# Moving transfers of a two-layer decoder step to ScalarE's DMA queue, and two cache copies to the middle of the last stage

## The chip, the cores and the metric

The kernel runs on one core of a Trainium2 chip. Five engines work side by side, each through its own instructions in order: TensorE (PE, with PEld for its weight loads), VectorE (DVE), ScalarE (ACT), GpSimd (POOL) and SyncE (SP), which only issues DMAs here. A DMA is an instruction on the engine that issues it: if it must wait for a tile to be free or for data to be ready, whatever stands behind it on that engine waits too. "SPq" and "ACTq" in the profile are DMA issues by SP and ScalarE.

The metric is the device time of one execution in microseconds (us). A second figure, the span, is the part of one profiled execution between its first and last instruction.

## What is computed

The reference is one inference step of a two-layer decoder on a prompt of 2048 tokens and a sample group of 8 x 4 tokens, in f32. Cut to what matters:

```python
for layer in range(DEPTH):                       # DEPTH = 2
    if layer < N_A_LAYERS:                       # mixer A: gated linear attention
        dp, st_p = gla_mixer(hp, zero_state, *w)
        ds, st_s = gla_mixer(hs, state_gla[i], *w)
        hp, hs = hp + dp, hs + ds
        k_p, v_p = shared_kv(hp, kv_norm, w_k, w_v, k_norm, pos_p)
        k_new, v_new = shared_kv(hs, kv_norm, w_k, w_v, k_norm, pos_s)
        k_s = jnp.concatenate([cache_swa_k, k_new], axis=1)
        v_s = jnp.concatenate([cache_swa_v, v_new], axis=1)
    else:                                        # mixer B: sliding-window attention
        q_p, g_p = swa_query(hp, b_norm[j], b_w_in[j], b_q_norm[j], pos_p)
        hp = hp + swa_out(swa_banded(q_p, k_p, v_p, b_sinks[j]), g_p, b_w_out[j])
        q_s, g_s = swa_query(hs, b_norm[j], b_w_in[j], b_q_norm[j], pos_s)
        hs = hs + swa_out(attend(q_s, k_s, v_s, pos_s, kpos_s, b_sinks[j]), g_s, b_w_out[j])

def swa_out(o, gate, w_out):                     # the last stage: (2048 x 2048) @ (2048 x 1024)
    return (o.reshape(bsz, seq_len, BRANCH_WIDTH) * jax.nn.silu(gate)) @ w_out

# also returned, besides hp and hs: the states of mixer A, the last keys and values of the prompt, and
new_cache_swa_k_sample = k_s[:, seq_s:]          # the old cache without its first 4 rows, then 4 new rows
new_cache_swa_v_sample = v_s[:, seq_s:]
```

## The kernel before

All products run in pairs of f16 numbers (a high and a low part), three passes for one f32 product. Activations are held transposed, 128 tokens (a chunk) at a time; there are 16 chunks.

The stages follow one another in this order:

1. **Mixer A**, four heads of four blocks of 512 tokens. Its gated result goes out to DRAM as `ogd[c]`, one tensor for each chunk.
2. **Mixer A's output product** (`a_out`, L1052). For each chunk four transposed loads (L1059, `v` or `sg` <- `ogd`) bring the result back with the contracted dimension on the partitions; two products of 48 matmuls follow, into the banks `pj` and `o`; VectorE adds the residual (L1066), the sum `h` is stored as `hd[c]` (L1067), and `norm_T` (L298) squares, scales, splits and transposes it for mixer B into `uT`. Beside this run the steps of the list `prep`: they load the weights of mixer B, convert them to pairs and store them in DRAM. Last in that list is `form_steps` (L849): the output weights of mixer B are combined for a product in Strassen's manner, with seven products in place of eight. For each of eight block rows it loads four raw tiles (L857, into two tiles `wraw` and the tiles `qT` and `kT`), forms seven combinations on GpSimd (L864), splits each on ScalarE and VectorE (L197, L198) and stores it as `wfd[n]` by GpSimd's queue.
3. **Mixer B's attention**, four groups of 16 chunks, `ORDER` (L1522) interleaving the scores and values of one chunk with the projections of a later one. The probabilities are transposed by DMA through SP (L1285, `sth` and `pst` <- `v`). The result goes to DRAM as `ogd2[c]`. The attention of the samples lies between the groups.
4. **The passage to the last stage**, the last loop steps `n = TOT` to `TOT + 2` with `TOT` = 64: TensorE still works on the attention of the last chunks and fills in with the first products of the last stage. The lists `trickle` and `summing` hand out loads of factors and of blocks, and VectorE's sums, a step at a time.
5. **The last stage**, mixer B's output product, a `Pair` of two chunks at a time. For a pair, four blocks `x` = 0 to 3 are loaded transposed (L1569, `load` and `fetch`), VectorE and ScalarE build the operands of the seven products from them (`sums`), and TensorE runs seven products of 24 matmuls each (`PRODS`) with the factors `wf[0]` to `wf[6]`. Factors come by `wform_big` (L1533, a tile of the ring `uT`) or `wform` (L1538, four tiles of the ring `W`). `Pair.y` finishes one half chunk: it loads the residual (L1625), VectorE adds it (L1626) and the product (L1618), and the result is stored (L1627). `b_finish_s` (L1664 to L1670) does the same for the samples.

What sets the order: the program is written in the order above with priorities (`behind` lowers one), and a planner then arranges the instructions of each engine by its own estimate of their times. So an instruction may be issued far ahead of the place where it is written. TensorE's order alone is fixed to that of the program while `pin[0]` is set, from the start of mixer B to the end of the passage. `later` (L108) keeps a DMA in its place in program order. Tiles are rings of buffers: a tag with `bufs` = 2 gives the third user the first one's memory, and a write into it waits until the last reader is done.

Places that the change touches: the raw loads (L857); the residual and the results (L1625, L1627, L1667, L1670); the copies of the caches without their first rows (two DMAs from DRAM to DRAM by L108) and of the sixteen pieces with the new rows (L1748, from `kvS`), all written after the loop of the passage; the blocks 0 and 1 of pair 0, which are loaded at `TOT - 11` into a shared tile of the ring `uT` for the early products and once more by `pairs[0].load` for the sums; and the steps at which the factors 2 and 6 are loaded.

Of the kernel before, what the change touches and what calls it, by code (L numbers as in the profile page):

```python
# [19 lines left out]
P = 128  # L20
# [10 lines left out]
NS, TS = 8, 4  # L31
SMP = NS * TS
WIN = 128
# [41 lines left out]
def _body(tc, nc, cp, sb, ps, dr, i, o):  # L75
# [6 lines left out]
    def T(tag, shape, dt, bufs=None):  # L82
        return sb.tile(shape, dt, tag=tag, name=nm(tag), **({} if bufs is None else {"bufs": bufs}))
# [4 lines left out]
    def C(tag, shape, dt):  # L88
        return cp.tile(shape, dt, tag=tag, name=tag)
# [16 lines left out]
    def later(dst, src, q=nc.sync):  # L106

        tc.keep_in_program_order(q.dma_start(dst, src))  # L108
# [30 lines left out]
    kvS = C("kvS", [SMP, 2, NKV, HD], F32)  # L139


    hsd = dr.tile([SMP, D], F32, tag="hsd", name="hsd")
# [5 lines left out]
    hd = [dr.tile([P, D], F32, tag=f"hd{c}", name=f"hd{c}") for c in range(NCH)]  # L148
# [15 lines left out]
    def run(steps):  # L164
        for f in steps:
            f()
# [7 lines left out]
    def behind(steps, n):  # L174


        def one(f):
            with tc.high_priority(offset=-n):
                f()

        return [lambda f=f: one(f) for f in steps]
# [8 lines left out]
    def split(dst, src, sc=None, eng=dve):  # L190

        hi, lo = dst
        if sc is None:
            act(hi, src, AF.Copy)  # L194
            eng.tensor_tensor(lo, src, hi, ALU.subtract)  # L195
        else:
            act(hi, src, AF.Copy, scale=sc)  # L197
            dve.scalar_tensor_tensor(lo, src, sc, hi, ALU.mult, ALU.subtract)  # L198

    class Unit:  # L200


        def __init__(self, parts, ncol, gs, kts, groups=0):
            self.ncol, self.t, self.pre, self.groups = ncol, None, None, groups
            self.parts, self.gs, self.kts = parts, gs, list(kts)
# [643 lines left out]
    def form_steps(m):  # L849

        b, f = {}, {}

        def load():
            for n, (r, z) in enumerate(((0, 0), (0, 1), (1, 0), (1, 1))):
                t = T(("wraw", "wraw", "qT", "kT")[n], [P, 512], F32, 3 if n < 2 else 1)
                k = UP[m] + 2 * r
                nc.sync.dma_start(t, i["b_w_out"][0][k * P : (k + 1) * P, z * 512 : z * 512 + 512])  # L857
                b[r, z] = t
            f[0], f[3], f[5] = b[0, 0], b[1, 0], b[1, 1]

        def put(n):
            def sub(x, y):
                t = T("sth", [P, 512], F32, 2)
                pool.tensor_tensor(t, x, y, ALU.subtract)  # L864
                f[n] = t

            if n == 2:
                sub(b[0, 1], b[0, 0])
            elif n == 1:
                sub(b[1, 1], f[2])  # L870
            elif n == 4:
                sub(b[1, 1], b[0, 1])
            elif n == 6:
                sub(b[1, 0], f[1])
            t = T(tags[0], [P, 2, 512], F16, 2)
            tags.append(tags.pop(0))
            split((t[:, 0], t[:, 1]), f[n], SWB)
            nc.gpsimd.dma_start(wfd[n][:, m], t)

        return behind([load] + [lambda n=n: put(n) for n in (0, 2, 1, 3, 6, 5, 4)], 200)  # L880
# [660 lines left out]
    quarters = lambda f, n: [lambda x=x: f(n, x) for x in range(4)]  # L1541
# [7 lines left out]
    def ring(kind, tags_, shape, dt):  # L1549
        tag = tags_[turn[kind] % len(tags_)]  # L1550
        turn[kind] += 1
        return T(tag, shape, dt, BUFS.get(tag, 2))

    class Pair:
        def __init__(self, p):
            self.p, self.r, self.l = p, {}, {}
# [64 lines left out]
        def y(self, c, half, pp, t):  # L1621

            cs = slice(half * 512, half * 512 + 512)
            hr = T("E", [P, 512], F32, 2)
            nc.sync.dma_start(hr, hd[c][:, cs])  # L1625
            dve.tensor_tensor(hr, hr, t, ALU.add)  # L1626
            nc.sync.dma_start(o["y"][0, c * P : (c + 1) * P, cs], self.add("st", pp, hr))  # L1627

        def steps(self, n):
            tag, w = PRODS[n]  # L1630
# [33 lines left out]
    def b_finish_s(half, pt):  # L1664
        cs = slice(half * 512, half * 512 + 512)
        hr = T("E", [SMP, 512], F32, 2)
        nc.sync.dma_start(hr, hsd[:, cs])  # L1667
        y = T("st", [SMP, 512], F32, 2)
        dve.tensor_tensor(y, pt, hr, ALU.add)
        nc.sync.dma_start(o["ys"].flatten_outer_dims()[:, cs], y)  # L1670

    blks = []
    parts = {}
# [1 line left out]
    pairs = [Pair(p_) for p_ in range(NCH // 2)]  # L1675
    TOT = NKV * NCH
    trickle, summing = [], []

    def s_out(half):

        cols = [slice(z * P, (z + 1) * P) for z in range(4)]
        right = [k + 2 for k in UP]
        fs, kts = ((0, 2, 5), UP + UP + right) if half else ((0, 3), UP + right)
        return out_sample([lambda k, hl, z=z: wf[fs[k // 8]](k % 8, hl, z) for z in cols], half, b_finish_s, kts, OSCB)

    for t in range(-3, NKV * NCH):
        fill = []
        n = t + 3
        if n < NKV * NCH:
            g, c = divmod(n, NCH)  # L1690
            blk = BBlk(g, c, gw[g], blks[-1] if c else None)
            blks.append(blk)
            fill = blk.steps()
            parts[n] = blk.attend_steps()
            if c == (SMC if g + 1 < NKV else 0):
                sm = SampleB(g, gw[g])
                boundary += [lambda sm=sm: run(sm.proj_steps())] + sm.steps()
        elif n < NKV * NCH + 3:
            fill = (pairs[0].steps(0) + pairs[0].steps(1), pairs[1].steps(0) + pairs[1].steps(1), s_out(0) + pairs[0].steps(2))[n - TOT]
        lists = {  # L1700
            "A": list(parts[t + 1][0]) if t + 1 in parts else [],
            "B": list(parts.pop(t)[1]) if t in parts else [],
        }
        nf = ORDER.count("f")
        seen = done = 0
        for x in ORDER:
            if x == "f":
                seen += 1
                upto = len(fill) * seen // nf
                run(fill[done:upto])  # L1710
                done = upto
                if trickle and seen % 3 == 0:
                    trickle.pop(0)()
                if boundary and seen == 7 and n > TOT - NCH + 3:
                    boundary.pop(0)()
                if summing and seen % 6 == 3 and (n > TOT or seen > 12):
                    summing.pop(0)()
            elif lists[x]:
                lists[x].pop(0)()
        if n < NKV * NCH and c == 12:  # L1720
            if g + 1 < NKV:
                run(gw[g + 1].steps())
        if n == TOT - 11:
            t_ = T("uT", [P, 8, 8, P], F16, 4)
            for x in range(4):
                pr = pairs[x // 2]
                pr.l[x % 2] = [t_[:, 2 * x], t_[:, 2 * x + 1]]
                pr.fetch(x % 2, pr.l[x % 2])
        if n in (TOT - 7, TOT - 3):
            run(quarters(wform_big, {TOT - 7: 0, TOT - 3: 2}[n]))  # L1730
        if n == TOT - 14:
            run(quarters(wform, 3))
        if n == TOT - 1:
            trickle += [lambda x=x: pairs[0].load(x) for x in (3, 2, 0, 1)] + quarters(wform_big, 1)
            summing += pairs[0].sums()
        if n == TOT:
            trickle += quarters(wform, 4) + quarters(wform, 5)
        if n == TOT + 1:
            trickle += quarters(wform_big, 6)
        if boundary:  # L1740
            boundary.pop(0)()
    for n, (od, ca) in enumerate((("cks", "cache_swa_k"), ("cvs", "cache_swa_v"))):
        later(o[od][:, : WIN - TS], i[ca][:, TS:])

    pin[0] = False
    for n, od in enumerate(("cks", "cvs")):
        for b in range(NS):
            nc.sync.dma_start(o[od][b, WIN - TS :], kvS[b * TS : (b + 1) * TS, n])  # L1748
    run(trickle + summing)
    for p_ in range(NCH // 2):  # L1750
        more = []
        if p_ + 1 < NCH // 2:
            nxt = pairs[p_ + 1]
            ld, sm = [lambda x=x, nxt=nxt: nxt.load(x) for x in (2, 3, 0, 1)], nxt.sums()
            more = ld[:2] + sm[:2] + ld[2:3] + sm[2:6]
        weave([f for n in range((3, 2, 0)[min(p_, 2)], 7) for f in pairs[p_].steps(n)], more)
        if more:
            run(ld[3:] + sm[6:])
        if p_ == 5:
            run(s_out(1))  # L1760

# [82 lines left out]
```

## Time and profile before

| | us |
|---|---|
| median of 3 runs | 2862.65 |
| lowest and highest | 2855.01, 2867.41 |
| the profiled execution | 2863.85 |
| its span | 2862.1 |

The mean clock granted to TensorE in the profiled execution is 0.983 of full speed. Its DMA queues, as the third part of the page gives them (packets, MB, share of the time of 16 DMA engines):

```profile
q1 hardware_dynamic: 761016, 352.75, 54.6%
q0 software_dynamic: 10880, 35.66, 3.4%
...
q10 hardware_dynamic: 2080, 0.07, 0.0%
```

Queue q1 is SP's, q0 is GpSimd's, and q10 holds the two small loads that ScalarE issues at the very start. All the large traffic on SP's queue is thus issued by one engine, in one order.

In what follows a timeline gives start and duration in us from the start of the span, engine, line of the kernel, operation, tiles (out<-in), the count of merged instructions, and in brackets the idle time of the engine just before with what ended it. A table of waits gives total us, number of times and the longest. A window gives its length and then, engine by engine, busy us with the number of instructions, the granted clock, the share of time that the 16 DMA engines were busy (packets in flight together count, so it can exceed 1) and GB/s.

### The profile page before, as it was taken

The page shows a single profiled execution, that of the slowest core. Times are in us where ns is not written, and L with a number is a line of the kernel's source. Part 1 is how long each engine was busy: PE and PEld are TensorE (multiplying, and loading weights), DVE is VectorE, ACT ScalarE, POOL GpSimd, SP SyncE. Part 2 cuts the span into 40 slices and gives each one's busy share as a digit, 9 for nine tenths or more (in the row PEclk, how much of TensorE's full clock was granted, in tenths as well). Part 3 has the DMA queues.
Part 4 walks back from the last instruction along what each step waited for, and adds up shares of the span by engine and source line. Part 5 has one row for each costly group of instructions (what it writes and reads, how often), then busy time and mean ns, then how long its engine had stood idle before and what let it go on. Part 6 is the DMA issues. An engine that isn't in the chain of part 4 may idle for free.

```text
span 2862.1 us, 51609 instructions
## 1 busy us (share of the span) xinstructions
PE 2735.9 (96%) x19070; PEld 1392.4 (49%) x19070; DVE 1845.7 (64%) x3815; ACT 1440.3 (50%) x3385; POOL 1063.6 (37%) x1471
## 2 busy tenths in 40 slices
PE   6899999999999999999899999999999999988999
PEld 3445444444454444444344555555555555543444
DVE  5767787677768775336413666677777766767653
ACT  6655665466546654333313555566666666641110
POOL 1242233222322321116405676666566556530000
PEclk9899999999999999999999999999999999999999
DMA  8351334124312533799975555866877788798651
GB/s 209 90 124 36 100 101 150 38 82 136 115 38 85 171 84 96 180 240 282 233 193 135 108 130 120 203 117 129 173 116 130 157 155 165 151 236 172 125 112 57
DMA packets 774230, 391.78 MB, mean 137 GB/s; under 512 B 629200, under 2 KB 698776, under 8 KB 773944
## 3 DMA queue, kind: packets, MB, share of 16 engines
q1 hardware_dynamic: 761016, 352.75, 54.6%
q0 software_dynamic: 10880, 35.66, 3.4%
q8 instruction: 149, 2.44, 0.4%
q14 instruction: 105, 0.86, 0.1%
q10 hardware_dynamic: 2080, 0.07, 0.0%
HBM read 138.90 MB, written 107.54 MB: 86 GB/s over the span
## 4 chain that ended last, share of the span: by engine, by line
PE 56%; DVE 12%; DMA 11%; ACT 10%; issue 6%; POOL 4%; SPq 1%; DVEq 0%; ACTq 0%; POOLq 0%
PE pj L101 33%; PE o L101 11%; PE tr L101 8%; PE kv L101 3%; ACT o L1279 2%; DMA pst<-v 2%; DVE v L198 2%; ACT v L197 2%; DMA pre<-pst 1%; PE lev L101 1%; DMA wraw<-in_a_w_in_dram 1%; DVE o L1274 1%; DVE W L198 1%; POOL ogT L195 1%; DVE lev L1274 1%
## 5 line engine op out<-in xcount | busy, mean ns | idle before, releaser
L101 PE MATMUL pj<-W,uT 128*128 128x512 f16 x5088 | 1208.1, 383 | 6.6 <-ACT qT L430 2.9
L101 PEld LDWEIGHTS <-uT 128*128 128x128 f16 x6976 | 654.7, 99 | 714.1 <-issue 40.4
L101 PE MATMUL tr<-W,uT 128*128 128x512 f16 x1536 | 365.8, 379 | 0.0
L186 POOL TENSOR_SCALAR rs_m<-ss 128x1 f32<-128x1 f32 (+3 forms) x190 | 46.1, 243 | 685.7 <-ACT og L611 234.0
L101 PEld LDWEIGHTS <-X 128*128 128x128 f16 x2744 | 185.8, 98 | 149.3 <-issue 14.7
L1279 ACT ACTIVATE o<-o,mx 128x256 f32<-128x256 f32 (+1 forms) x384 | 168.5, 439 | 168.1 <-DVE mx L1274 163.6
L1274 DVE CUSTOM_DVE_ANT_0 o<-o,madd,nsink 128x256 f32<-128x256 f32 (+1 forms) x384 | 184.0, 479 | 48.3 <-PE o L101 44.0
L101 PE MATMUL pj<-uT,W 128*128 128x512 f16 (+1 forms) x912 | 186.0, 354 | 27.0 <-DMA uT<-ogT 24.3
L198 DVE SCALAR_TENSOR_TENSOR v<-o,v 128x512 f16<-128x512 f32 (+1 forms) x192 | 128.8, 671 | 102.0 <-ACT v L197 82.0
L187 POOL TENSOR_TENSOR rs_r<-rs_m,mhalf 128x1 f32<-128x1 f32 (+2 forms) x186 | 184.8, 994 | 14.4
L101 PEld LDWEIGHTS <-W 128*128 128x128 f16 x2448 | 128.0, 98 | 113.1 <-issue 18.5
L101 PEld LDWEIGHTS <-v 128*128 128x128 f16 x976 | 95.2, 98 | 116.0 <-DMA v<-ogd 1.9
L508 POOL TENSOR_TENSOR E<-bt 128x256 f32<-128x256 f32 x96 | 73.9, 770 | 198.4 <-DVE X L195 124.8
L195 POOL TENSOR_TENSOR ogT<-og,ogT 128x512 f16<-128x512 f32 x68 | 88.0, 1295 | 154.4 <-ACT ogT L194 142.5
L101 PEld LDWEIGHTS <-sth 128*128 128x128 f16 x2080 | 111.4, 99 | 52.3 <-DMA sth<-v 12.2
L101 PEld LDWEIGHTS <-sg 128*128 128x128 f16 x800 | 78.6, 99 | 107.5 <-DMA sg<-ogd 12.3
L101 PE MATMUL o<-gl,X 128*128 128x256 f16 (+1 forms) x768 | 114.9, 273 | 5.5 <-DMA X<-qe 5.5
L197 ACT ACTIVATE v<-o 128x512 f16<-128x512 f32 (+1 forms) x192 | 111.3, 579 | 11.1 <-DMA sth<-v 7.6
L101 PE MATMUL kv<-rmask,sth 128*128 128x64 f16 x1984 | 107.0, 194 | 10.1 <-DMA sth<-v 9.2
L101 PE MATMUL kv<-rmask,pst 128*128 128x64 f16 x992 | 102.4, 194 | 9.3 <-DMA pst<-v 9.3
L1279 ACT ACTIVATE lev<-lev,mx 128x256 f32<-128x256 f32 (+1 forms) x128 | 56.5, 441 | 103.3 <-DVE mx L1274 101.2
L101 PE MATMUL pj<-W,v 128*128 128x512 f16 x448 | 104.2, 379 | 1.1 <-DMA v<-ogd 1.1
(468 smaller groups left out, 5092.5 us busy)
## 6 DMA issues: line engine op xcount, KB each, us to landing
pre<-pst POOLq DMA_DIRECT2D x72, 256.0 KB, 3.4
W<-pre SPq DMA_DIRECT2D x36, 512.0 KB
ogd<-ogT SPq DMA_DIRECT2D x68, 256.0 KB
wraw<-in_a_w_in_dram SPq DMA_DIRECT2D x64, 256.0 KB
wraw<-in_b_w_in_dram SPq DMA_DIRECT2D x64, 256.0 KB
oge<-ogT SPq DMA_DIRECT2D x64, 256.0 KB
wraw<-in_a_w_out_dram SPq DMA_DIRECT2D x32, 256.0 KB
X<-in_x_prompt_dram SPq DMA_DIRECT2D x32, 256.0 KB
```

The lines of the kernel that those rows point to most:

```text
L101: return order(nc.tensor.matmul(*a, **k))
L186: pool.tensor_scalar(m[:n, :k], ss, a, b, ALU.mult, ALU.add)
L187: pool.tensor_tensor(r[:n, :k], m[:n, :k], mhalf[:n, :k], ALU.pow)
L195: eng.tensor_tensor(lo, src, hi, ALU.subtract)
L197: act(hi, src, AF.Copy, scale=sc)
L198: dve.scalar_tensor_tensor(lo, src, sc, hi, ALU.mult, ALU.subtract)
L508: pool.tensor_tensor(Ev[:, :, 0, :], ref, btv[:, :, 0, :], ALU.subtract)
L1274: dve.tensor_tensor_reduce(pm[:, z], pm[:, z], madd.rearrange("p a b -> p (a b)")[:, (2 - nk) * P :], -0.125, nsink[:, g * GRP + h : g * G ...
L1279: act(pm[:, z], pm[:, z], AF.Exp, scale=-1.0, bias=nm_[:, h : h + 1], accum_out=bx["sum"][:, h : h + 1])
```

## The change

Raw output weights (L857), residual and results of the last stage, and the sample's pair of transfers are issued by ScalarE. `out_q` switches the queue of `Pair.y` once the passage is over, so the first half chunk of pairs 0 and 1, written before, stays with SP. The cache copies and the sixteen pieces are written after pair 3 and issued by ScalarE. Blocks 0 and 1 of pair 0 are taken for the sums from the shared tile (`pr.r[x] = pr.l[x]`) and their second load is left out. Factor 2 is loaded one chunk earlier, and factor 6, whose tile is the shared one, is loaded after the sums of pair 0.

```diff
@@ form_steps
-                nc.sync.dma_start(t, i["b_w_out"][0][k * P : (k + 1) * P, z * 512 : z * 512 + 512])
+                nc.scalar.dma_start(t, i["b_w_out"][0][k * P : (k + 1) * P, z * 512 : z * 512 + 512])
@@ before class Pair
+    out_q = [nc.sync.dma_start]
@@ Pair.y
-            nc.sync.dma_start(hr, hd[c][:, cs])
+            out_q[0](hr, hd[c][:, cs])
             dve.tensor_tensor(hr, hr, t, ALU.add)
-            nc.sync.dma_start(o["y"][0, c * P : (c + 1) * P, cs], self.add("st", pp, hr))
+            out_q[0](o["y"][0, c * P : (c + 1) * P, cs], self.add("st", pp, hr))
@@ b_finish_s
-        nc.sync.dma_start(hr, hsd[:, cs])
+        nc.scalar.dma_start(hr, hsd[:, cs])
         y = T("st", [SMP, 512], F32, 2)
         dve.tensor_tensor(y, pt, hr, ALU.add)
-        nc.sync.dma_start(o["ys"].flatten_outer_dims()[:, cs], y)
+        nc.scalar.dma_start(o["ys"].flatten_outer_dims()[:, cs], y)
@@ the loop over attention and the passage
             for x in range(4):
                 pr = pairs[x // 2]
                 pr.l[x % 2] = [t_[:, 2 * x], t_[:, 2 * x + 1]]
+                if x < 2:
+                    pr.r[x] = pr.l[x]
                 pr.fetch(x % 2, pr.l[x % 2])
-        if n in (TOT - 7, TOT - 3):
-            run(quarters(wform_big, {TOT - 7: 0, TOT - 3: 2}[n]))
+        if n in (TOT - 7, TOT - 4):
+            run(quarters(wform_big, {TOT - 7: 0, TOT - 4: 2}[n]))
...
-            trickle += [lambda x=x: pairs[0].load(x) for x in (3, 2, 0, 1)] + quarters(wform_big, 1)
+            trickle += [lambda x=x: pairs[0].load(x) for x in (3, 2)] + quarters(wform_big, 1)
...
-        if n == TOT + 1:
-            trickle += quarters(wform_big, 6)
...
-    for n, (od, ca) in enumerate((("cks", "cache_swa_k"), ("cvs", "cache_swa_v"))):
-        later(o[od][:, : WIN - TS], i[ca][:, TS:])
-
     pin[0] = False
-    for n, od in enumerate(("cks", "cvs")):
-        for b in range(NS):
-            nc.sync.dma_start(o[od][b, WIN - TS :], kvS[b * TS : (b + 1) * TS, n])
-    run(trickle + summing)
+    run(trickle + summing + quarters(wform_big, 6))
+    out_q[0] = nc.scalar.dma_start
@@ the loop over pairs, after the products of pair p_
+        if p_ == 3:
+            for n, (od, ca) in enumerate((("cks", "cache_swa_k"), ("cvs", "cache_swa_v"))):
+                later(o[od][:, : WIN - TS], i[ca][:, TS:], nc.scalar)
+                for b in range(NS):
+                    nc.scalar.dma_start(o[od][b, WIN - TS :], kvS[b * TS : (b + 1) * TS, n])
```

## The prediction

> **What bounds the kernel now.** The page's first part comes first: who is busy, over which span.
>
> ```profile
> span 2862.1 us, 51609 instructions
> PE 2735.9 (96%) x19070; PEld 1392.4 (49%) x19070; DVE 1845.7 (64%) x3815; ACT 1440.3 (50%) x3385; POOL 1063.6 (37%) x1471
> ```
>
> TensorE is the bound; no matmul is added or removed, so all that can come back is its idle time, 2862.1 - 2735.9 = 126.2 us, and the slow matmuls behind long idle times. The profiled run took 2863.85 us, 1.75 above its span and 1.2 above the median, 2862.65. Next I read the windows of the stages that the change touches (columns: length, then busy us and instructions of PE, PEld, DVE, ACT, POOL, granted clock, DMA share, GB/s).
>
> ```profile
> 1280.00:1400.00 120.00, 107.88 (x710) 51.66 (x708) 69.06 (x76) 44.80 (x84) 74.90 (x92) 0.94 1.00 272
> 2520.00:2630.00 110.00, 91.75 (x647) 45.83 (x644) 74.27 (x143) 33.48 (x82) 13.97 (x17) 0.91 0.97 217
> 2630.00:2858.00 228.00, 228.00 (x1227) 106.16 (x1224) 121.70 (x195) 27.95 (x49) 0.00 (x0) 1.00 0.46 104
> 1800.00:2500.00 700.00, 676.24 (x6177) 385.94 (x6174) 496.59 (x1309) 438.59 (x1331) 434.95 (x553) 0.99 0.76 149
> ```
>
> The first is mixer A's output product with the conversion of the output weights beside it: 12.1 us idle, DMA engines full. The second is the passage into the last stage: 18.25 us idle, DMA engines nearly full. In the third TensorE never stops, so faster transfers there are worth nothing. The fourth is attention.
>
> Where the 12.1 us lie, from the timeline of TensorE (start, duration, group, in brackets the idle time before it) and two narrower windows:
>
> ```profile
> 1353.83 10.52 PE L101 MATMUL pj<-W,v 128*128 128x512 f16 x48
> ...
> 1384.07 1.04 PE L101 MATMUL pj<-W,sg 128*128 128x512 f16 x2 [9.36 <-DMA sg<-ogd]
> 1386.64 12.60 PE L101 MATMUL pj<-W,sg 128*128 128x512 f16 x46 [1.54 <-DMA sg<-ogd]
> ```
>
> ```profile
> 1370.00:1380.00 10.00, 4.71 (x22) 1.96 (x20) 7.17 (x8) 4.20 (x8) 7.83 (x10) 0.90 0.73 219
> 1380.00:1390.00 10.00, 4.40 (x10) 1.32 (x11) 3.34 (x6) 3.28 (x7) 6.20 (x8) 0.50 1.22 264
> ```
>
> One hole: 9.36 + 1.54 = 10.9 us, waiting for the transposed loads sg<-ogd. Behind it the clock is 0.50, and 46 matmuls take 12.60 us where 48 took 10.52 (0.219 each): 46 x 0.219 = 10.1, so 2.5 us more are lost. While TensorE waited, the DMA share was 0.73. So the engines had room, and the transposes were late because SP had not issued them:
>
> ```profile
> 1363.27 0.53 SPq L857 DMA_DIRECT2D kT<-in_b_w_out_dram  x1
> 1363.85 0.93 SPq L857 DMA_DIRECT2D wraw<-in_b_w_out_dram  x2
> 1371.60 0.33 SPq L857 DMA_DIRECT2D qT<-in_b_w_out_dram  x1
> 1372.75 0.33 SPq L1067 DMA_DIRECT2D hd<-E  x1
> ...
> 1375.50 5.38 SPq L1059 DMA_TRANSPOSE sg<-ogd  x2
> ```
>
> ```profile
> 1369.25 1.19 DVE L198 SCALAR_TENSOR_TENSOR pst<-kT,pst 128x512 f16<-128x512 f32 x1 [5.33 <-ACT pst L197]
> ...
> 1372.05 0.68 DVE L1066 SCALAR_TENSOR_TENSOR E<-pj,X 128x512 f32<-128x512 f32 x1
> ```
>
> From 1364.8 to 1371.6 SP stands at a raw weight load (L857) until its tile is free: 6.8 us. Then it stands at the store of h (L1067), which waits for VectorE's L1066, itself 5.33 us late behind a weight split that waited for the raw kT; and kT was issued only at 1363.27, since it too queued on SP. The raw loads thus hold the transposes up twice.
>
> In the second stretch, TensorE's waits (engine and line, what it waited for: total us, times, longest):
>
> ```profile
> PE kv L101 <- DMA pst<-v: 5.7, 3, 3.8
> PE o L101 <- DVE st L1618: 4.5, 1, 4.5
> PE tr L101 <- DVE st L1669: 3.7, 1, 3.7
> PE kv L101 <- DMA sth<-v: 3.0, 1, 3.0
> PE pj L101 <- DMA uT<-wf: 0.8, 1, 0.8
> ```
>
> The 4.5 us at bank o hang on the cache copies: the SP queue, the chain of waits (start, us, what) and VectorE, in that order.
>
> ```profile
> 2589.96 0.81 SPq L108 DMA_DIRECT2D out_cks_dram<-in_cache_swa_k_dram  x1
> ...
> 2593.00 9.78 SPq L1569 DMA_TRANSPOSE v<-oge  x1
> ```
>
> ```profile
> 2591.63 13.61 DMA pst<-oge
> ...
> 2609.19 4.95 DMA sg<-oge
> ```
>
> ```profile
> 2605.33 1.29 DVE L1583 TENSOR_TENSOR wraw<-sth,pst 128x512 f32<-128x512 f16 x2 [5.91 <-DMA pst<-oge]
> ```
>
> The transpose issued right behind the two cache copies takes 13.61 us against 4.95 for a later one, the next needs 9.78 us merely to issue, and VectorE, which makes the sums of pair 1 and empties the banks, loses 5.91 us.
>
> **The change, part by part.**
>
> *Raw output weights on ScalarE's queue.* 32 issues leave SP; the 6.8 us stop goes with them, and kT can start before the two u transposes that it followed, which shortens the chain to L1067 as well. I take the sg transposes 8 us earlier: 10.9 becomes about 3, and most of the 2.5 us of slow clock goes: gain 9 for an upper end of 10.9 + 2.5 = 13.4. The lower end is 0 (DMA engines full all the same) or below (rivals). What is late next is the store of h, no longer held by raw loads. The cost moves to ScalarE:
>
> ```profile
> SPq L857 <- POOL sth L864: 9.3, 6, 6.7
> ...
> SPq L857 <- DVE pst L198: 4.4, 2, 3.5
> ```
>
> ```profile
> L857 SPq DMA_DIRECT2D wraw<-in_b_w_out_dram x16: 328/422/788, 1276.5 to 1381.0; - x16
> ```
>
> ```profile
> L133 ACTq DMA_DIRECT2D gsa<-in_a_norm_dram x1: 460/460/460, 0.7 to 0.7; - x1
> ```
>
> The only kind of issue on ScalarE that the trace shows took 0.46 us, like SP's median 0.42. So 32 x 0.42 = 13.4 us of issue and up to 9.3 + 4.4 = 13.7 us of waits come to an engine that is busy 44.8 of 120 us. Behind a waiting load stand norm_T's squares and splits and the weights' own splits; TensorE's banks here are emptied by VectorE. Taken at nothing, covered by one chunk (96 matmuls, 21 us) of spare banks and tiles; without that cover, 27.1 us.
>
> *Caches copied later.* The 8.7 us (13.61 - 4.95) leave the chain: the 4.5 at bank o should go, with the slow clock behind it. In these windows TensorE is slow or waiting:
>
> ```profile
> 2590.00:2600.00 10.00, 10.00 (x40) 4.22 (x39) 9.12 (x16) 3.69 (x6) 0.00 (x0) 0.84 1.19 237
> ...
> 2620.00:2630.00 10.00, 6.57 (x23) 2.67 (x23) 10.00 (x18) 1.67 (x3) 0.00 (x0) 0.83 0.26 84
> ```
>
> Lost to the clock: 10 x 0.16 = 1.6 us behind the 3.7 us wait, 6.57 x 0.17 = 1.1 behind the 4.5. I take 4.5 + 1.1, rounded to 5.5. The copies land in the stretch that is 0.46 full, with TensorE covered by tiles loaded a pair ahead: nothing there. The 16 copies of new rows go to ScalarE as well; they may be planned early:
>
> ```profile
> L1748 SPq DMA_DIRECT2D out_cvs_dram<-kvS x8: 280/316/504, 2362.3 to 2402.1; - x8
> ```
>
> Though written behind the loop, they were issued in attention. On ScalarE 16 x 0.46 = 7.4 us at most; ScalarE is 63% busy there (438.59 of 700). I charge 1.
>
> *Residual and results on ScalarE.* 60 issues at 0.42 make 25 us on an engine busy 27.95 of 228; its other work there, one bank copy a pair and the splits of the next pair, is needed at least four products (20 us) later. Nothing, covered by that. The sample's pair of transfers goes too; the 3.7 us wait at bank tr ended with this:
>
> ```profile
> DVE st L1669 <- DMA out_y_dram<-st: 5.3, 1, 5.3
> ```
>
> The tile was held by a y store. That one is still SP's (it is made before the switch), though with less ahead of it: I take 3 of 3.7 + 1.6, ends 0 and 5.3.
>
> *Two blocks not loaded twice.* Four transposes of 1.3 us go from SP, of which two fell in the full stretch:
>
> ```profile
> 2541.30 1.30 SPq L1569 DMA_TRANSPOSE qT<-oge  x1
> ```
>
> They lay ahead of the attention transposes (5.7 + 3.0 us of waits). I take 2.5, ends 0 and 8.7. Third factor 2 earlier: covered, nothing. Factor 6 now also waits for the sums to have read the shared tile:
>
> ```profile
> 2563.06 1.75 SPq L1533 DMA_DIRECT2D uT<-wf  x4
> ```
>
> ```profile
> 2563.32 1.04 DVE L1583 TENSOR_TENSOR wraw<-qT,kT 128x512 f32<-128x512 f16 x1
> ```
>
> It was issued at 2563.06, and that last read ends at 2564.4: 1.3 us later, with four products (20 us) that don't need it. Nothing; 0 to 5 if it lands behind the pair loads.
>
> Sum: 9 + 5.5 + 3 + 2.5 - 1 = 19. 2863.85 - 19 = 2844.85; less 1.2 for the median, 2843.7, say **2844**.
>
> The Trainium skill, page "DMA: Bandwidth & Descriptors", section "Issuing engines are not separate DMA queues", speaks against the first part: all issuing engines feed the same 16 DMA engines, so that a second one saves only the time to issue. By that rule the 9 falls out, which is the rival below. The same skill, "TensorE: Matmul & The Clock Gate", Part 1, says that an idle window of about 3.4 us halves the clock; the 0.50 after 9.36 us agrees, and by it closing a hole to 3 us saves its slow matmuls whole, as I count.
>
> **The rivals.**
>
> *Full DMA engines* (0.20). Share 1.00 over 1280 to 1400 speaks for it, 0.73 in the hole against: earlier transposes only queue behind other packets. The 9 falls out: 2844 + 9 = 2853.
>
> *Attention gives it back* (0.13). Moving DMAs re-plans the order, and the 16 small copies sit amid ScalarE's exponentials. TensorE's idle time there is 700 - 676.24 = 23.8; grown by half, 2844 + 11.9 = 2856.
>
> *ScalarE held up* (0.10), the other side. If norm_T falls behind by more than the 21 us of one chunk, tiles of h are not freed, VectorE cannot empty the banks, and the 27.1 us reach TensorE: 2862.65 + 27.1 - 10 (the last stage's part) = 2880. For it: in-order waits; against: 44.8 + 27.1 = 72 of 120 us.
>
> *Everything closes* (0.10). 13.4 + 18.25 + 2.7 = 34.4: 2828. For it, no other bound is near; against, three factors are still loaded around 2520.
>
> That the change does little of what it says is in the first rival.
>
> **How the numbers follow.** Forecast 0.47, its own range 2836 to 2852. A measurement can tell about 0.5%, 14.3 us: faster is below 2848.3. Of the forecast 0.38 lies there, with the last rival's 0.10 and a little of the first's: 0.50. Within: 0.40. Slower: 0.10. The range 2829 to 2866 leaves out the slow rival and most of the best one.
>
> **What would show it.** Right: no wait of TensorE over 3 us for sg<-ogd, clock above 0.9 there; no L857 on SP; pst<-oge near 5 us in the passage; at most 8 us idle in the 110 us of the passage. Wrong: that wait unchanged with DMA share near 1; ScalarE waiting at L857 while VectorE waits for ScalarE's ogT; more than 24 us idle in 700 us of attention; TensorE waiting for factor 6.

## The result, and the profile after

| | kernel before | changed kernel |
|---|---|---|
| median | 2862.65 | 2903.13 |
| lowest and highest of 5 runs | 2855.01, 2869.13 | 2902.49, 2907.88 |
| the profiled execution, its span | 2863.85, 2862.1 | 2907.88, 2906.1 |

The changed kernel is slower: ratio 1.0146, 95% interval 1.013 to 1.0162. In its lines, those from `class Pair` on stand two further down (L1618 is now L1620, L1626 is L1628, L1569 is L1571, L1669 is L1671).

The first part of the page shows the same work in a longer span: TensorE is busy as long as before, and 169 us idle where it was 126.

```profile
span 2906.1 us, 51595 instructions
PE 2737.1 (94%) x19070; PEld 1392.6 (48%) x19070; DVE 1847.2 (64%) x3815; ACT 1439.4 (50%) x3385; POOL 1062.5 (37%) x1471
```

The windows of mixer A's output stage, of attention (30 us later than before), of the passage and of the last stage, first of the changed kernel, then of the kernel before (attention's row of before stands in the prediction):

```profile
1280.00:1440.00 160.00, 122.59 (x757) 57.30 (x755) 73.68 (x85) 47.55 (x90) 76.34 (x99) 0.89 1.11 226
1830.00:2530.00 700.00, 674.66 (x6144) 384.24 (x6141) 497.02 (x1307) 436.09 (x1327) 434.31 (x551) 0.99 0.75 149
2520.00:2640.00 120.00, 106.78 (x850) 58.12 (x849) 83.64 (x180) 49.79 (x133) 32.03 (x39) 0.96 0.95 199
2640.00:2800.00 160.00, 141.26 (x639) 63.15 (x638) 94.13 (x152) 21.54 (x37) 0.00 (x0) 0.95 0.62 121
```

```profile
1280.00:1440.00 160.00, 146.74 (x892) 69.33 (x890) 82.33 (x99) 56.06 (x107) 81.28 (x105) 0.96 0.99 254
2520.00:2640.00 120.00, 101.75 (x693) 50.34 (x690) 81.36 (x154) 34.64 (x85) 13.97 (x17) 0.91 0.95 211
2640.00:2800.00 160.00, 160.00 (x912) 75.52 (x911) 96.94 (x157) 21.59 (x38) 0.00 (x0) 1.00 0.55 115
```

Idle time plus busy time times the missing clock gives what each window lost. Mixer A: 37.4 + 122.59 x 0.11 = 50.9, before 13.3 + 5.9 = 19.1, so **31.8 lost**. The passage: 13.2 + 4.3 = 17.5, before 18.2 + 9.2 = 27.4, so **9.9 won**. The last stage: 18.7 + 7.1 = **25.8 lost**, from nothing. Attention is idle for 25.3 us where it was 23.8. Together 49, for spans that differ by 44.0 (the windows don't hold exactly the same work; the passage, too, lies some 32 us later, but its window holds all of its waits in both kernels).

**Mixer A.** SP no longer stops at L857, as foreseen; what got slower is the issue of its transposed loads (timeline of SP), and GpSimd waits for raw tiles (timeline of GpSimd):

```profile
1322.24 10.51 SPq L1059 DMA_TRANSPOSE sg<-ogd  x3
...
1350.50 19.76 SPq L1059 DMA_TRANSPOSE v<-ogd  x4
...
1386.24 14.26 SPq L1059 DMA_TRANSPOSE sg<-ogd  x3
```

```profile
1312.38 1.27 POOL L864 TENSOR_TENSOR sth<-kT,sth 128x512 f32<-128x512 f32 x1 [14.60 <-DMA kT<-in_b_w_out_dram]
...
1367.80 1.26 POOL L864 TENSOR_TENSOR sth<-kT,sth 128x512 f32<-128x512 f32 x1 [8.52 <-DMA kT<-in_b_w_out_dram]
```

Three transposed loads took 10 to 14 us to issue and four took 19.76; before, two took 4.85 to 5.81 and three 7.68. A long issue alone doesn't cost time, though: in raw_gps, a run below that loses nothing, three took up to 16.52. All waits of GpSimd for raw tiles, and how often, from the view by source line of L857, first after, then before:

```profile
  POOL sth L864: 48.2, 7
```

```profile
  POOL sth L864: 16.4, 6
```

The splits of the weights on ScalarE and VectorE depend on GpSimd's combinations, and between these splits stand the residual's additions and `norm_T`, on which SP's order waits. The table of TensorE's waits over the whole run shows what this costs (before: 10.9 for `sg<-ogd`, nothing over 4.5 at a bank):

```profile
PE pj L101 <- DMA sg<-ogd: 25.6, 4, 9.5
...
PE pj L101 <- DVE st L1620: 18.7, 2, 10.9
...
PE pj L101 <- DMA v<-ogd: 9.2, 4, 5.2
```

**The last stage** has two holes, 7.85 and 10.89 us, together the 18.7. The second, from the timelines of ScalarE, VectorE, SP and TensorE:

```profile
2733.75 0.72 ACTq L108 DMA_DIRECT2D out_cks_dram<-in_cache_swa_k_dram  x1
2734.57 0.48 ACTq L1627 DMA_DIRECT2D E<-hd  x1
...
2754.40 0.69 DVE L1628 TENSOR_TENSOR E<-E,kT 128x512 f32<-128x512 f32 x1 [17.96 <-DMA E<-hd]
...
2740.13 15.68 SPq L1571 DMA_TRANSPOSE sg<-oge  x1
...
2755.93 1.01 PE L101 MATMUL pj<-W,v 128*128 128x512 f16 x2 [10.89 <-DVE st L1620]
```

The residual's load, issued right behind the copy of the k cache, lands 19.8 us later; VectorE waits for it with the next bank behind it; and a transposed load on the other queue takes 15.68 us to issue. (The v cache's copy, written at the same place, was planned into attention, at 2406.9.) What sort of copy this is, the DMA view of 2733 to 2755 us shows:

```profile
DMA packets 2795, 2.39 MB, mean 109 GB/s; under 512 B 2393, under 2 KB 2393, under 8 KB 2779
...
q10 hardware_dynamic: 455, 1.81, 63.1%
...
out_cks_dram<-in_cache_swa_k_dram ACTq DMA_DIRECT2D x1, 992.0 KB
```

16 packets are longer than 8 KB, as many as there are DMA engines: 992 / 16 = 62 KB each. ScalarE's queue took 63.1% of 16 x 22 us = 222 us, so the 16 packets took at most 13.9 us each on average.

### The profile page after: what moved, and what is told of

Read it like the earlier page. It is cut to its first block, busy times and chain, and to the rows that moved or that the text cites. A ratio compares the mean times of both kernels' runs of the same rounds, so it can differ in the third digit from the quotient of the medians.

```text
span 2906.1 us, 51595 instructions
## 1 busy us (share of the span) xinstructions
PE 2737.1 (94%) x19070; PEld 1392.6 (48%) x19070; DVE 1847.2 (64%) x3815; ACT 1439.4 (50%) x3385; POOL 1062.5 (37%) x1471
## 4 chain that ended last, share of the span: by engine, by line
PE 52%; DMA 13%; DVE 12%; ACT 10%; issue 7%; POOL 5%; SPq 1%; ACTq 0%; DVEq 0%; POOLq 0%
PE pj L101 31%; PE o L101 9%; PE tr L101 8%; PE kv L101 3%; ACT o L1279 2%; DVE v L198 2%; ACT v L197 2%; DMA pre<-pst 1%; PE lev L101 1%; DMA pst<-v 1%; DMA kT<-in_b_w_out_dram 1%; DVE o L1274 1%; DMA wraw<-in_a_w_in_dram 1%; DMA E<-hd 1%; DMA sth<-v 1%
## 5 line engine op out<-in xcount | busy, mean ns | idle before, releaser
L1274 DVE CUSTOM_DVE_ANT_0 o<-o,madd,nsink 128x256 f32<-128x256 f32 (+1 forms) x384 | 183.8, 479 | 46.9 <-PE o L101 42.5
L101 PE MATMUL pj<-W,v 128*128 128x512 f16 x448 | 108.4, 389 | 27.9 <-DVE st L1620 18.7
L101 PE MATMUL kv<-rmask,sth 128*128 128x64 f16 x1984 | 106.1, 194 | 11.7 <-DMA sth<-v 10.9
L101 PE MATMUL pj<-W,sg 128*128 128x512 f16 x368 | 92.2, 396 | 25.6 <-DMA sg<-ogd 25.6
```

The lines of the kernel that those rows point to most:

```text
L101: return order(nc.tensor.matmul(*a, **k))
L1274: dve.tensor_tensor_reduce(pm[:, z], pm[:, z], madd.rearrange("p a b -> p (a b)")[:, (2 - nk) * P :], -0.125, nsink[:, g * GRP + h : g * G ...
```

## The experiments

Unless said otherwise a run differs from the kernel before; ratios are to it, with 95% intervals. "Waits for ogd" are TensorE's for `v` and `sg` between 1270 and 1450 us, 12.0 before and 34.8 in the changed kernel.

### Which part costs what

**raw_only** and **raw_back**: the raw loads alone, in both directions.

```diff
 raw_only:  kernel before       raw_back:  changed kernel
-nc.sync.dma_start(t, i["b_w_out"]...)      -nc.scalar.dma_start(t, i["b_w_out"]...)
+nc.scalar.dma_start(t, i["b_w_out"]...)    +nc.sync.dma_start(t, i["b_w_out"]...)
```

> The kernel before with only the raw output weights on ScalarE's queue. Theory, two queues in flight: plain loads on ScalarE's ring beside SP's transposed loads slow each other, and that alone makes the loss in mixer A, about 28 us: 2891 us, raw loads landing 12 to 18 us after issue, transposes of ogd issuing for 5 to 20 us, GpSimd waiting over 40 us for them at L864. Rival, ScalarE held up: about as late (2880 to 2891), but raw loads land in about 5 us once issued, and what is late is norm_T's ogT from a ScalarE that waits at L857. Rival, the loss comes only from the parts together (last stage included): within 10 us of 2863.

> The changed kernel with only the raw output weights back on SP. Two queues in flight, with terms that add up: 2903 - 28 = 2875 us; the two holes of the last stage (7.9 and 10.9 us) stay, the waits for ogd in mixer A go back to about 12 us. If the parts hang together: still over 2890.

Measured: 2878.16, 1.0065 (1.0044 to 1.0086), and 2884.46, 1.0074 (1.0057 to 1.009). Alone the raw loads cost 0.65%, 18.6 us; put back they return 2903.1 - 2884.5 = 18.7 (by the ratios 0.72%, 20.6 us). The terms add up, to about two thirds or three quarters of the 28 us expected; raw_back lies 9 us above its 2875. The waits for ogd are 23.2 in raw_only; in raw_back the two holes of the last stage stay, 7.1 and 9.3 us. The view by source line of raw_only shows no long semaphore record of ScalarE at such a load (durations in ns, least, median, most):

```profile
L857 ACTq EVENT_SEMAPHORE  x18: 17/17/17, 1273.9 to 1406.6; - x18
```

Such records alone don't settle it: before, SP's longest at L857 is 3.5 us, though SP stood there for 6.7. But in ScalarE's timeline from 1265 to 1420 us the gaps ahead of these loads add up to only 3.9 us, the longest 1.48, and to 2.5 in the changed kernel. So the waits that SP had at L857 did not move to ScalarE, and "ScalarE held up" as the prediction had it is out.

**results_only** (`out_q` and the sample's pair on ScalarE) and **blocks_only** (the two blocks, factors 2 and 6): those parts of the change alone, with the caches where they were.

> The kernel before with only residuals and results of the last stage, and the sample's pair, on ScalarE's queue; the caches are copied where they were, on SP. If the hole of 10.9 us is made by the cache copies ahead of the residual's load in ScalarE's ring, it is absent here, and if the hole of 7.9 us is made by the residual's load beside transposed loads, it is there: 2863 + 8 + slow clock, 2870 to 2876. Rival, as predicted: the queue costs nothing and the wait of 3.7 us for the sample's tile goes: 2860.

> The kernel before with only the two blocks not loaded twice, factor 2 loaded earlier and factor 6 after the sums; all on SP. The prediction's term: 2.5 us off, ends 0 and 8.7, factor 6 costing 0 to 5: 2857 to 2865. In the changed kernel factor 6 was waited for 2.8 us: that wait should be here too.

Measured: 2866.98, 1.0013 (0.9998 to 1.0028), and 2861.46, 0.9997 (0.9984 to 1.0011): neither can be told from no change. results_only has no hole like the two: its longest wait after 2500 us is 4.3, at bank o, where it was 4.5 before. In the passage the sample's wait is still there in results_only, and factor 6 is waited for in blocks_only (a row of the table of TensorE's waits in the one, of its timeline in the other):

```profile
PE tr L101 <- DVE st L1671: 3.0, 1, 3.0
```

```profile
2570.67 1.01 PE L101 MATMUL pj<-uT,S 128*128 128x512 f16 x2 [2.29 <-DMA uT<-wf]
```

**caches_back**: raw_back with the caches copied in the passage again, on SP.

```diff
-        if p_ == 3: ... later(o[od][:, : WIN - TS], i[ca][:, TS:], nc.scalar) ...
+    for n, (od, ca) in ...: later(o[od][:, : WIN - TS], i[ca][:, TS:])      # ahead of pin[0] = False
```

> The changed kernel with the raw weights back on SP and the caches copied where they were before, on SP: what is left is results on ScalarE and the two blocks. If the copy on ScalarE's ring makes the hole of 9 to 11 us (the residual's load lands 18 us after issue, behind the copy), that hole goes: 2884 - 9 - 3 of slow clock = 2872. The hole of 7 us, where loads of the residual come one after the other, then stays if it belongs to results and blocks together; if it too is the copy's, 2861 to 2866.

Measured: 2861.91, 0.9999 (0.9981 to 1.0017), the time of the second case. Moving the caches thus costs 1.0074 - 0.9999 = 0.75%, some 21 us, the other half of the loss. The second hole is gone; of the first, waits of 4.1 at bank pj and 2.5 at bank o are left.

### The caches: a place in a ring, or long packets

**caches_gps** was to copy them at the same place by GpSimd's queue:

> The changed kernel with the raw weights back on SP, the caches copied at the same place but on GpSimd's queue (the small copies on SP). If the residual's load is late because it stands behind the copy in one ring, it lands in under 6 us and the hole of 9 to 11 us goes: 2872. If the copy slows everything in flight beside it, whatever its ring, transposed loads and the residual's load stay slow and the hole stays over 5 us: 2878 to 2884.

It doesn't answer: the planner issued the k cache's copy at 2567.6, in the passage. Its 10 runs lie in two groups, 2853 to 2854 and 2865 to 2883; 1.003 (1.0004 to 1.0057).

**caches_pieces**: raw_back with the k cache's copy in eight pieces, around the same two residual loads on ScalarE's ring. Ring and bytes are the same and the packets are shorter; besides, ScalarE now issues the copy over 8 us, with half of it ahead of the first of these loads.

```diff
-later(o["cks"][:, : WIN - TS], i["cache_swa_k"][:, TS:], nc.scalar)
+for b in range(NS):
+    nc.scalar.dma_start(o["cks"][b, : WIN - TS], i["cache_swa_k"][b, TS:])   # behind the load of hd[c0]
```

> The changed kernel with the raw weights back on SP, and the copy of the k cache in the last stage in 8 pieces with packets of 8 KB, in place of one copy with 16 packets of 62 KB; same ring, same bytes, ahead of the same two residual loads. If the residual's load is late because 16 long packets keep all 16 DMA engines for some 15 us each, whatever stands behind them in either ring: it lands within 8 us and the hole of 9 to 11 us is under 3 us, 2872 to 2878. If standing behind 1 MB in one ring is enough: the hole stays, 2884.

Measured: 2866.25, 1.0014 (1.0 to 1.0028), so 0.60% or 17 us of the 21 come back. From the DMA view of 2694 to 2715 us and VectorE's timeline:

```profile
DMA packets 7447, 4.18 MB, mean 199 GB/s; under 512 B 6550, under 2 KB 6550, under 8 KB 7446
...
out_cks_dram<-in_cache_swa_k_dram ACTq DMA_DIRECT2D x8, 124.0 KB
```

```profile
2704.89 0.69 DVE L1629 TENSOR_TENSOR E<-E,kT 128x512 f32<-128x512 f32 x1 [2.94 <-DMA E<-hd]
```

The load (issued at 2698.76) lands within 6.1 us though it stands behind half of the pieces in one ring; the next load, behind all of them, is not waited for; and the longest issue of a transposed load near them is 3.40 us. The second hole is gone: after the first, of 8.31 us, which ends at 2634.57, TensorE waits no more. So it is the copy in one piece that costs, and neither its ring nor its bytes. That the length of its packets does it, and not that its bytes come all at once, is the likely reading, but no run takes the two apart.

**spread**: blocks_only with the caches on SP in pieces, one of each cache a pair, from the third pair; it leaves out the last two of eight pieces of both caches.

> The kernel before with the two blocks not loaded twice, and the caches copied in 8 pieces each through the last stage, two pieces a pair from the third, all on SP. If the prediction's gain for the passage was right but lost by the place and ring of the copy: no wait over 2 us at bank o in the passage, no hole in the last stage, 2863 - 5.5 - 2.5 = 2855. Rival, other waits close the passage: 2859 to 2863.

Measured: 2862.81, 1.0 (0.9983 to 1.0017). The wait at bank o is gone, but factor 6 is waited for 4.2 us, and bank pj 3.8.

### The raw loads: whose queue

Every run of this table changes only the queues of the raw loads (L857) and of the stores of the finished weights (L878):

```diff
-nc.sync.dma_start(t, i["b_w_out"]...)
+nc.<loads>.dma_start(t, i["b_w_out"]...)
-nc.gpsimd.dma_start(wfd[n][:, m], t)
+nc.<stores>.dma_start(wfd[n][:, m], t)
```

| run | loads | stores | queues in mixer A | median | ratio | waits for ogd | GpSimd's waits for raw tiles |
|---|---|---|---|---|---|---|---|
| before | SP | GpSimd | 2 | 2861 | | 12.0 | 16.4 |
| raw_only | ScalarE | GpSimd | 3 | 2878.16 | 1.0065 (1.0044 to 1.0086) | 23.2 | 42.5 |
| raw_gps | GpSimd | GpSimd | 2 | 2854.73 | 0.9983 (0.9966 to 1.0) | 4.0 | 15.1 |
| both_act | ScalarE | ScalarE | 2 | 2861.24 | 0.9999 (0.9982 to 1.0016) | 5.1 | 21.5 |
| raw_act_stores_sp | ScalarE | SP | 2 | 2856.19 | 0.9988 (0.9974 to 1.0001) | 5.0 | 25.0 |
| raw_gps_stores_act | GpSimd | ScalarE | 3 | 2865.71 | 1.0022 (1.0 to 1.0043) | 11.5 | 26.9 |

The theory after the first call was that any second queue beside SP's transposed loads slows them:

> The kernel before with only the raw output weights on GpSimd's queue, where also the finished weights are stored. Two queues in flight: transposed loads again issue for 5 to 20 us while plain loads are under way, TensorE waits for ogd more than 20 us in mixer A, 2875 or more. ScalarE held up (its waits at L857 are what costs): ScalarE has no such wait here, so 2855 to 2864; GpSimd's own waits, if they cost, show as waits for sth and not for ogd.

It fell: with GpSimd's queue the waits shrink. The next was that ScalarE's queue in particular slows SP's. **copies_act** and **copies_gps** add 16 copies of 256 KB that nobody waits for, to a scratch in DRAM (`dum`):

```diff
+                if n in (0, 3):
+                    later(dum[2 * m + n // 3], i["b_w_out"][0][...], nc.scalar)    # copies_gps: nc.gpsimd
```

> The kernel before, its raw weights on SP, with 16 further copies of 256 KB (two for each of the 8 rounds of weights, from the raw weights to a scratch in DRAM that nobody reads) on ScalarE's queue. Nothing waits for them, so only what is in flight can slow. If ScalarE's ring slows SP's: SP's packets take over 40 ns each in mixer A (37.5 before, 44 with the raw weights on ScalarE), transposed loads issue for 8 us and more, TensorE waits for ogd over 20 us: 2875 or more. If the loss comes from the place of the raw loads in ScalarE's or the planner's order: the extra bytes cost a little, under 2870, SP's packets stay near 37 ns.

> The same 16 further copies on GpSimd's queue instead. If it matters which ring carries them: SP's packets stay near 35 ns, as with the raw weights on GpSimd (34), and the time is at least 8 us below that of the copies on ScalarE's. If only the bytes count: both the same within 4 us.

Measured: 2866.47, 1.0027 (1.0012 to 1.0043), and 2868.2, 1.0033 (1.0016 to 1.0051): the same. Between 1280 and 1400 us SP's packets took 69.3% of 16 x 120 us for 33297 of them, 40.0 ns each; worked out in the same way 39.6 before, 46.7 in raw_only and 35.6 in raw_gps (the expectation's figures are for 20 us more). So that theory fell too. The traces speak against it even more than the times: TensorE's waits for ogd are 10.5 with the copies on ScalarE's queue and 24.0 with them on GpSimd's, where SP's packets took 41.9 ns. Left was the count of queues in flight:

> The kernel before with the raw output weights and also the stores of the finished ones on ScalarE's queue, none on GpSimd's: two rings carry mixer A's transfers as before. If a third ring in flight is what costs (raw weights on ScalarE beside SP's transposed loads and GpSimd's stores, each taking its turn): the raw loads land in 5 to 7 us again, TensorE waits for ogd under 15 us, 2855 to 2866. If ScalarE's place costs (loads stand behind what waits there): worse than the raw loads alone on ScalarE, since its stores wait for VectorE too: 2880 or more.

> The kernel before with the raw output weights on GpSimd's queue and the stores of the finished ones on ScalarE's: three rings in flight, and the raw loads where GpSimd frees their tiles. A third ring: 2870 to 2885, raw loads landing over 9 us after issue. ScalarE's place for the loads: 2850 to 2860, as with the raw weights alone on GpSimd, or somewhat more for what the stores hold up.

> The kernel before with the raw output weights on ScalarE's queue and the stores of the finished ones on SP's: two rings, and the loads at the same place of ScalarE as in the changed kernel. A third ring: the loads land in under 9 us, and TensorE waits for ogd less than the 23 us with the raw weights alone on ScalarE; SP's own stores hold its transposed loads up, so 2860 to 2872. ScalarE's place: loads land as late as there, 2878 or more.

Measured: see the table. raw_act_stores_sp leaves the loads on ScalarE as the change has them, and moves only GpSimd's stores, to SP's queue: the whole loss is gone. The windows of raw_only, then of raw_act_stores_sp, then of raw_gps:

```profile
1280.00:1440.00 160.00, 132.25 (x801) 62.37 (x800) 76.40 (x86) 47.75 (x91) 75.61 (x99) 0.90 1.10 229
```

```profile
1280.00:1440.00 160.00, 154.59 (x930) 73.06 (x928) 79.09 (x101) 56.98 (x109) 53.69 (x50) 0.98 1.05 270
```

```profile
1280.00:1440.00 160.00, 154.50 (x936) 73.55 (x934) 77.83 (x96) 53.39 (x104) 92.86 (x130) 0.99 1.03 247
```

The last two columns are the point: the share adds up the time of all packets in flight. For each 100 GB/s it is 1.10 / 2.29 = 0.48 in raw_only and 0.49 in the changed kernel, but 0.39 to 0.42 before and in the three runs of the table with two queues, and 0.43 in raw_gps_stores_act. With the loads on ScalarE's queue beside SP's and GpSimd's, packets thus take a seventh to a quarter more time for the same bytes, and transfers land later: GpSimd's stores in raw_only a median 7.9 to 8.6 us after issue, 4.7 to 6.4 before. GpSimd's waits for raw tiles are longest there too; the length of SP's issues is no sign of the loss (in both_act four transposed loads took 15.80).

The count of queues is not the whole rule, though. copies_act has three in flight as well, and there the share is 1.07 / 2.74 = 0.39, and mixer A loses 19.7 us by the sum used above, 19.1 before; copies_gps has two and loses 34.5. A third queue cost time here when it carried loads or stores of the chain that TensorE waits for, and not when it carried copies that nobody waits for. That the queues take turns at the engines is argued, not shown. That GpSimd is relieved of its stores is not what helps: in raw_gps_stores_act it is relieved too, and by the medians that run is 11 us slower than raw_gps, in which GpSimd is busiest (92.86 us) and nothing is lost. Yet its 2865.7 is less than the 2870 expected of a third queue: three queues cost most when ScalarE's carries the loads on which the conversion waits. Why that much more, the runs don't tell.

### A version that beats both, and the first hole

**gps_and_pieces**: raw loads on GpSimd's queue, caches on SP in pieces, two of each cache after each of the pairs 1 to 4. **pieces_blocks** and **pieces_results** add to it the edits of blocks_only and of results_only.

```diff
-nc.sync.dma_start(t, i["b_w_out"]...)
+nc.gpsimd.dma_start(t, i["b_w_out"]...)
+        for n, (od, ca) in ...:                          # after the products of pair p_
+            for b in range(2 * p_ - 2, 2 * p_) if 1 <= p_ <= NS // 2 else ():
+                later(o[od][b, : WIN - TS], i[ca][b, TS:])
```

> A candidate: the kernel before with the raw output weights on GpSimd's queue, and the caches on SP in 8 pieces each, out of the passage, over pairs 1 to 4 of the last stage. If the two gains add: 2855 (the raw weights alone) less up to 5.5 for the passage: 2849 to 2855. If attention or the passage gives the second back: 2855 as before.

> The kernel with raw weights on GpSimd's queue and the caches in pieces (2847), with the two blocks not loaded twice, factor 2 earlier and factor 6 after the sums. If these edits make the wait of 7 to 8 us at bank pj about 70 us into the last stage (absent without them in that kernel, 3.8 in the kernel with blocks and pieces alone): a wait of 3 us or more there, 2849 to 2856. If they are what the prediction said: no such wait, 2843 to 2847.

> The same kernel (2847) with residuals and results of the last stage and the sample's pair on ScalarE's queue instead. If the wait at bank pj comes from residual loads that go one after the other on ScalarE's ring: 3 us or more there, 2850 to 2856. If results on ScalarE cost nothing, as predicted: no such wait, 2843 to 2849.

Measured: 2847.32, **0.9957 (0.9942 to 0.9971)**, faster than both kernels; 2853.88, 0.9969 (0.9956 to 0.9982); and 2851.22, 0.9961 (0.9942 to 0.998). The windows of gps_and_pieces in mixer A and the last stage:

```profile
1280.00:1440.00 160.00, 152.84 (x934) 72.77 (x933) 79.89 (x97) 53.60 (x106) 93.02 (x130) 1.00 1.04 245
...
2640.00:2800.00 160.00, 159.65 (x910) 75.28 (x909) 93.15 (x151) 22.28 (x40) 0.00 (x0) 1.00 0.53 113
```

The wait at bank pj is absent in gps_and_pieces and pieces_results, 0.8 in results_only, 2.6 in blocks_only and in pieces_blocks (just under the 3 expected, with 4.4 for factor 6), 3.8 in spread, 4.1 in caches_back, and 7.1 to 8.3 where results are on ScalarE and the copies are out of the passage as well (raw_back, caches_pieces, the changed kernel). So the blocks' edit (with its factors 2 and 6) makes it. That residual loads on ScalarE stretch it, where two loads one after the other took 3.2 and 5.9 us in the changed kernel's chain, is argued, not shown. The times of the three kernels can't be told apart by their intervals.

## Why the prediction was wrong, point by point

- **Raw output weights on ScalarE's queue**, gain 9: measured a loss of 18.6. This term has the wrong sign. Its first half held: SP lost the issues and the stop. The step that failed is "I take the sg transposes 8 us earlier": it counted SP's order and ScalarE's instructions, but the loads' own landing not at all. Its premise, that the engines had room while TensorE waited, was read ahead of the hole: the share of 0.73 is that of 1370 to 1380 us, but the wait of 9.36 us runs from 1374.7 to 1384.1, where the share is 1.08 (the prediction's next row, 1380 to 1390, has 1.22). What came in place of the gain: on ScalarE's queue, beside SP's and GpSimd's, the loads landed late. GpSimd's waits for raw tiles at L864 went from 16.4 to 48.2 us, and TensorE's for ogd from 12.0 to 34.8. Why three queues do this is open. The rival "Full DMA engines" saw the DMA share of 1.00 and rightly doubted the gain, but gave it zero and not a loss.
- **Caches copied later**, gain 5.5 and nothing in the last stage: measured a loss of 21 for the whole edit. The failing step is "the copies land in the stretch that is 0.46 full, with TensorE covered by tiles loaded a pair ahead: nothing there". A mean share of 0.46 tells nothing of 16 packets that take up to 13.9 us each on average, and the residual's tiles are not loaded a pair ahead: `E` has two buffers. The profile showed the price already: the 13.61 us behind the same copies in the passage, which the prediction took as a matter of place. The passage itself gained nearly as foreseen: 9.9 where 5.5, 3 and 2.5 were counted, though 13.2 us of it stay idle and not 8.
- **Residual and results on ScalarE**, nothing: right as far as 0.13% (-0.02 to 0.28) can be told. The 3 us for the sample's tile are not this edit's: the wait stays at 3.0 in results_only.
- **Two blocks not loaded twice**, gain 2.5: 0.03% (-0.11 to 0.16), no gain seen. Factor 6 came late, 2.3 to 4.4 us, inside the 0 to 5 named. A wait of 2.6 to 3.8 us at bank pj was not foreseen.
- **Attention gives it back**: 25.3 idle in place of 23.8, not the 11.9 more of that rival.
- **ScalarE held up**, 2880, was the right side for the wrong reason: the gaps of ScalarE ahead of its loads at L857 add up to 2.5 us, where that rival moved 13.7 us of waits there. It was the only case above the range, and at 0.10 the side on which the time fell had too small a chance.

The prediction cited the Trainium skill, "DMA: Bandwidth & Descriptors", section "Issuing engines are not separate DMA queues": a second issuing engine saves only the time to issue. The runs agree that nothing more is won and add that much can be lost. The same page, section "Queues, rings and completion order", says that a DMA engine takes turns between the queues that have work and drains a whole packet before it switches. Both losses fit that rule, if a third queue takes turns from the other two and 62 KB packets make long turns. No trace here shows the turns, and copies_act, whose third queue costs mixer A nothing, shows that the rule alone doesn't give the size of the loss.

## What to carry to other kernels

Before a transfer is moved to another queue, count the queues that are in flight in that stretch and ask what waits for each transfer in it. Here the loads on which the conversion waits cost 0.65% on a third queue, and nothing that can be told in the three runs with only two. Look at the packets of a large copy before its place: cut into eight pieces, the copy of 1 MB held up nothing that TensorE waited for; in 16 packets it held up the loads of two queues.

## What the runs showed of the hardware

- A copy of 992 KB from DRAM to DRAM in 16 packets of 62 KB delayed a 256 KB load behind it in its ring to 18 to 20 us and the issue of a transposed load in another ring to 14 to 16 (1.23 to 1.45 by the medians). In eight pieces, with packets under 8 KB: 6.1 and 3.4.
- With raw loads on ScalarE's queue beside SP's transposed loads and GpSimd's stores, packets took a seventh to a quarter more time for the same bytes (0.48 to 0.49 of share for 100 GB/s against 0.39 to 0.42 with two queues). With copies on ScalarE's queue that nobody waits for, it stayed at 0.39.
- On GpSimd's queue the raw loads landed a median 5.9 us after issue in raw_gps, and the waits for ogd fell from 12.0 to 4.0. By the time, this run can't be told from those with loads on ScalarE's queue and no third one.
